# A decoder block with 32 experts on one core: how many weight tiles the experts' stage requests ahead of its products

## The chip, the cores and the metric

One core of one Trainium2 chip runs the kernel. The metric is device microseconds (us) of one execution, lower is better. The kernel before took 1326.5 us (median of 3 runs, 1325.47 to 1329.25). Five engines work side by side: TensorE (PE, matrix products), VectorE (DVE), ScalarE (ACT), GpSimd (POOL) and SyncE (SP, which here only issues transfers). Each runs its own instructions in order and waits on semaphores for the others.

## What is computed

One layer of a transformer decoder, in f32, for T = 1024 tokens of D = 1024 numbers: two kinds of attention, an output projection with a residual, and then a mixture of 32 experts. The part that matters here is the last one; cut from the reference:

```
h2 = modulate(rmsnorm(x, g_ffn), shift_ffn, scale_ffn)          # (1024, 1024)
group  = argmax(softmax(h2 @ w_group))                          # 1 of 4
top 2 of the group's 8 experts, weights p1, p2 (times the group's probability)
y[t]   = sum over the token's 2 experts e of  weight * (silu(h2[t] @ w_gate[e]) * (h2[t] @ w_up[e])) @ w_down[e]
x      = x + gate_ffn * y ;   return rmsnorm(x, g_final)
```

Each expert has three weight matrices of 1024 x 512 (gate, up) and 512 x 1024 (down), 6 MB together. Which tokens an expert gets is known only once the routing is done.

## The kernel before, in words

**The stages.** Attention takes the first 600 us or so. Then comes the out-projection with the residual and the routing (the profile shows it until about 742 us), then the experts' stage (742 to 1290 us), then the final norm. The change is in how many of the experts' weights are requested in the second of these and how many are held ahead in the third.

**The weights.** The weights of an expert are 12 tiles of 128 x 1024 numbers (512 KB): eight (`ew<e>_0` to `_7`) hold gate and up, four (`_8` to `_11`) hold down. There are 384 such tiles. The function `load_to(n)` (from L971) issues the next tiles until n of them have been requested, each with one transfer on SP's queue (L982, "ew<-we" in the profile). The tiles are requested in the order in which the products use them. For experts 4 and up the place in memory is read from a register, which SP loads first (L980).

**The slots.** Every tile is taken by `slot(name)` (L129) from one pool of `NSLOT = 49` slots of 4 KB per partition. The pool holds the weights and also the other large tiles of this stage: the gathered tokens `xe` (three, in turn), the transposed tokens `xs<e>`, the activations `sg<e>`, `act<e>`, `at<e>`, the results `ys<e>`, `yt<e>`, and the broadcast row `bc_gate2`. Slots are dealt out when the program is built, in the order in which the code asks for them. Whoever writes first into a slot waits, on the chip, until the last reader of the tile that had it before is done.

**Requests during the routing.** `end_units` lists the units of work of the out-projection stage. Between them, `spread` puts calls of `load_to`, so that after the n-th group of units `LDS[n]` tiles have been requested in all. Each of these early requests also waits for ACT's latest instruction at that place (`queue_after`, `act_now`) and for the landing of the request 14 places earlier (`PACE`).

**The experts' loop.** The token rows of the first experts are gathered by `load_x(0)`, `load_x(1)`, `load_x(2)` (GpSimd's indirect transfer, L1226). Requests made after `load_x(1)` wait for its gather. The loop then walks through a list `order` of steps: `G` e,i is the product of the i-th gate/up tile (`gate_up`, `products`), `X` e the transpose of the gathered tokens (`xpose`: PE L1259 into PSUM, then eight copies with scale and shift that ACT, L1247, and DVE, L1245, make in turn into `xs<e>`), followed by ACT's scaling of the next gathered rows (L1237), `T` e the transpose of the activations (`act_t`, PE L1310, ACT L1312), `D` e,f the product of the f-th down tile, and `Y` e the result (`finish`, DVE L1329, L1335), which GpSimd adds into memory (`add_rows`, L1342). After the last gate/up product, `gate_up` issues the activation: ACT L1295 (silu), L1282, L1300 and DVE L1296, L1283, L1301, L1302, each waiting for the one before. The list puts six of the next expert's G steps in front of X (`XA = 6`), four of them in front of T (`TA = 4`) and one between T and D (`DA = 5`). So with expert 0 the steps run: X0, G0.0 to G0.5, X1, G0.6, G0.7, G1.0 to G1.3, T0, G1.4, D0.0 to D0.3, Y0, G1.5, X2, and so on.

**The products.** An expert takes 96 rows (large) or 64 (small: 5, 7, ... 27, 30, 31). `products` multiplies the first 64 rows tile by tile (L1270). The last 32 rows of a large expert follow after every fourth tile for four tiles together (L1277), and only then are these four weight tiles given back to the pool, one after the other.

**The lead.** Before each G or D step, at position `wpos` of the 384, the loop asks for `wpos + LL` tiles, with `LL = LLX = 34` and `LT = 0`.

Of the kernel before, what the change touches and what calls it, by code (L numbers as in the profile page):

```python
# [38 lines left out]
RP, RU = 6, 0  # L39
PO = 1  # L40
PO2 = 22
LDS = [6, 6, 11, 14, 18, 22, 28, 33, 33, 34]
PACE = 14
TZ, DZ = 2, 3
W2 = [0, 0]
# [13 lines left out]
QS = "AS"  # L59
TAIL = "y s3 r0-4 o0 s4 s5 x o1 o2 s6 s7 o3 r4-9 o4 o5 o6 o7 o8"  # L60
XA, TA, DA = 6, 4, 5
LLX = 34
LT = 0
NT = 0
PLO = ()

# [29 lines left out]
def build(nc, tc, I, out, cap=CAP):  # L96
# [25 lines left out]
    def act_now():  # L122
        return next(i for i in reversed(nc.cur_bb.bb.instructions) if i.engine == mybir.EngineType.Activation)

    def queue_after(d, ins):
        tc.add_manual_dep(d.ins, ins.name, mybir.DependencyInfo(
            mybir.DependencyClass.Sync, mybir.DependencyReason.DATA), reason="order of transfers")

    def slot(name, dt=F32):  # L129
        return up.tile([128, D], dt, name=name, tag="u")  # L130

    def bank(name, shape=(128, 512)):
        return pB.tile(list(shape), F32, name=name, tag="b")
# [478 lines left out]
    def spread_row(name, col, eng):  # L612

        t = bc[name] = slot("bc_" + name)
        for h in (0, 1):
            ps = bank(f"bc_{name}{h}")
            for k in range(4 * h, 4 * h + 4):
                c = slice(k * 128, k * 128 + 128)
                if eng is A:
                    A.activation(t[:, c], ident, AF.Copy, scale=col[:, k:k + 1])  # L620
                else:
                    eng.tensor_scalar(t[:, c], ident, col[:, k:k + 1], None, op0=ALU.mult)
                PE.matmul(ps[:, c.start - h * 512:c.stop - h * 512], ones, t[:, c], start=True, stop=True)
            A.activation(t[:, h * 512:h * 512 + 512], ps, AF.Copy)
# [341 lines left out]
    wseq = [o for o in order if o[0] in "GD"]  # L966
    wpos = {o: n for n, o in enumerate(wseq)}
    loaded, after = [0], [None]

    def load_to(n):  # L970
        while loaded[0] < min(n, len(wseq)):  # L971
            kind, e, i = wseq[loaded[0]]
            c = i if kind == "G" else KT + i
            w = slot(f"ew{e}_{c}")
            cc = slice(c * 1024, (c + 1) * 1024)
            if e < NF:
                src = I["we"][e, :, cc]
            else:
                if i == 0 and kind == "G":
                    EREG[e] = nc.sync.value_load(permi[0:1, e:e + 1], min_val=0, max_val=NE - 1)  # L980
                src = I["we"][bass.ds(EREG[e], 1), :, cc].rearrange("o p c -> (o p) c")
            d = nc.sync.dma_start(w, src)  # L982
            if after[0] is None:
                queue_after(d, act_now())
                if len(fetched) >= PACE:
                    queue_after(d, fetched[-PACE])
                fetched.append(d.ins)
            else:
                queue_after(d, after[0])
                fetched.append(d.ins)  # L990
            EW[kind, e, i] = w
            loaded[0] += 1
# [53 lines left out]

    LOADS = LDS

# [176 lines left out]
    def load_x(e):  # L1225
        g = G.indirect_dma_start(out=XE[e % 3][:capof(e)], out_offset=None, in_=x1d[:],  # L1226
                                 in_offset=bass.IndirectOffsetOnAxis(ap=listof(e), axis=0),
                                 bounds_check=T - 1, oob_is_err=False)
        if e == 1:
            after[0] = g.ins  # L1230

    def scale_x(e):

        xe, c = XE[e % 3], capof(e)
        r2 = (lacc[:, 2 * NE:] if e < NF else wlP[:, NE:])[:c, e:e + 1]
        if e:
            A.activation(xe[:c], xe[:c], AF.Copy, scale=r2)  # L1237
        else:
            A.activation(xe[:c, 0:384], xe[:c, 0:384], AF.Copy, scale=r2)
            V.tensor_scalar(xe[:c, 384:1024], xe[:c, 384:1024], r2, None, op0=ALU.mult)  # L1240
# [8 lines left out]
    def xpose(e):  # L1249

        xe, c = XE[e % 3], capof(e)
        wl = lacc[:, NE:3 * NE] if e < NF else wlP
        st = ST[e] = dict(wt=wl[:c, e:e + 1],
                          x=slot(f"xs{e}")[:, :KT * c].rearrange("p (k t) -> p k t", k=KT))
        n = 512 // c // 4 * 4
        for k0 in range(0, KT, n):
            tp = bank(f"xp{e}_{k0}", (128, n, c))
            for k in range(k0, k0 + n):
                PE.transpose(tp[:, k - k0, :], xe[:c, k * 128:(k + 1) * 128], ident[:c, :c])  # L1259
            for k in range(k0, k0 + n):  # L1260
                affine(k, st["x"][:, k], tp[:, k - k0, :])
# [23 lines left out]
    def gate_up(e, k):  # L1285
        st, c = ST[e], capof(e)
        if k == 0:
            st["gu"] = wide(f"gu{e}")
        ps = st["gu"]
        products(ps, st["x"], e, "G", k, KT)  # L1290
        if k == KT - 1:
            act = st["act"] = slot(f"act{e}")[:, 0:512]
            tmp = slot(f"sg{e}")
            s = tmp[64:128, 0:512]
            A.activation(s, ps[0:64, 0:512], AF.Silu)  # L1295
            V.tensor_mul(act[0:64], s, ps[64:128, 0:512])  # L1296
            if c > 64:
                t, s = tmp[0:64, 0:512], tmp[32:64, 512:1024]
                others(t, ps)
                A.activation(s, t[0:32], AF.Silu)  # L1300
                V.tensor_mul(act[64:96], s, t[32:64])  # L1301
            V.tensor_scalar(act[:c], act[:c], st["wt"], None, op0=ALU.mult)  # L1302
            del st["gu"]

    def act_t(e):
        st, c = ST[e], capof(e)
        act = st.pop("act")
        tp = bank(f"ap{e}", (128, 4, c))
        for f in range(4):
            PE.transpose(tp[:, f, :], act[:c, f * 128:(f + 1) * 128], ident[:c, :c])  # L1310
        st["a"] = slot(f"at{e}")[:, 0:4 * c].rearrange("p (k t) -> p k t", k=4)
        A.activation(st["a"], tp, AF.Copy)  # L1312

    def down(e, f):
        st = ST[e]
        if f == 0:
            st["y"] = wide(f"y{e}")
        products(st["y"], st["a"], e, "D", f, 4)

    def finish(e):  # L1320
        st, c = ST.pop(e), capof(e)
        ps = st["y"]
        p0 = 64 if e == NE - 1 else 0
        ys = YL if e >= NE - 2 else slot(f"ys{e}")
        g = bc["gate2"]
        halves = [(slice(h * 512, h * 512 + 512), h) for h in (0, 1)]
        for n, h in halves:
            r = slice(h * 64, h * 64 + 64)
            V.tensor_mul(ys[p0:p0 + 64, n], ps[r, 0:512], g[r, n])  # L1329
        if c > 64:  # L1330
            t = slot(f"yt{e}")[0:64, 0:512]
            others(t, ps)
            for n, h in halves:
                r = slice(h * 32, h * 32 + 32)
                V.tensor_mul(ys[64:96, n], t[r], g[r, n])  # L1335
        if e < NE - 2:
            add_rows(e, ys)
        if e == NE - 3:
            f_load()
# [22 lines left out]
    def f_square(tt, x):  # L1362
        FY[tt] = slot(f"fy{tt}")
        A.activation(FY[tt], x, AF.Square, accum_out=ssf[:, tt:tt + 1])
# [8 lines left out]
            G.indirect_dma_start(out=out[:], out_offset=rows_l, in_=y, in_offset=None,  # L1373
                                 bounds_check=T - 1, oob_is_err=False)

    LL = LLX
    load_x(0)
    load_x(1)
    load_x(2)
# [6 lines left out]
    for o in order:  # L1386
        kind, e, i = o
        if kind in "GD":
            load_to(max(loaded[0], wpos[o] + LL - wpos[o] * LT // len(wseq)))
        if kind == "G":  # L1390
            gate_up(e, i)
        elif kind == "X":
            xpose(e)
            if e + 1 < NE:
                scale_x(e + 1)
            if e + 2 < NE:
                load_x(e + 2)
        elif kind == "T":
            act_t(e)
        elif kind == "D":  # L1400
            down(e, i)
        elif kind == "Y" and e < NE - 1:
            finish(e)
        if o == ("G", NE - 3, 4):

            spread_row("final", cols[:, 72:80], G)
            XL, YL = slot("xlast"), slot("ylast")
            ML = slot("same")[:, 0:128]
            G.memset(XL, 0.0)
            A.activation(ML, ident, AF.Copy, scale=lsLf)  # L1410
            mp = bank("same", (128, 128))
            PE.matmul(mp, ones, ML, start=True, stop=True)
            V.tensor_scalar(ML, mp, lsLf, None, op0=ALU.is_equal)
        if e == NE - 1 and kind == "D" and i:
            f_square(i - 1, FX[i - 1])
# [37 lines left out]
    with tc.If(rv > 0):  # L1453
# [5 lines left out]
        for tt in range(KT):  # L1459
            for c in (0, 1):  # L1460
                o, j, ov = wk[:, 0:32], wk[:, 32:64], wk[:, 64:65]
# [135 lines left out]
```

## Time and profile before

| | |
|---|---|
| Runs | 1325.47, 1326.5, 1329.25 us; median 1326.5 |
| Profiled execution, its own time | 1328.25 us |
| Its span in the trace | 1326.5 us |
| Granted PE clock, mean | 0.960 |
| PE busy | 1168.2 us, 88% of the span |
| DVE, ACT, POOL busy | 738.0, 530.5, 227.1 us |
| Transfers | 304.8 MB, mean 230 GB/s over the span |
| Experts' weights | 384 transfers of 512 KB, median 10.8 us to landing |

"Span" is the time between the first and the last instruction in the trace; the execution's own time is 1.75 us longer. In the chain that ended last, PE has 43% and DMA 23% of the span. A row "A <- B: x, n, y" of the waits says that A stood idle for x us in n waits, y the longest, each ended by B. In the timeline a row gives start, duration, engine, line, operation, out<-in, count, and in brackets the engine's idle time before it and what ended it. In the windows' rows, PEclk is the clock granted to PE as a share of full speed, and "DMA share" the mean busy share of the core's 16 DMA engines.

### The profile page before, as it was taken

The page shows a single profiled execution, that of the slowest core. Times are in us where ns is not written, and L with a number is a line of the kernel's source. Part 1 is how long each engine was busy: PE and PEld are TensorE (multiplying, and loading weights), DVE is VectorE, ACT ScalarE, POOL GpSimd, SP SyncE. Part 2 cuts the span into 40 slices and gives each one's busy share as a digit, 9 for nine tenths or more (in the row PEclk, how much of TensorE's full clock was granted, in tenths as well). Part 3 has the DMA queues.
Part 4 walks back from the last instruction along what each step waited for, and adds up shares of the span by engine and source line. Part 5 has one row for each costly group of instructions (what it writes and reads, how often), then busy time and mean ns, then how long its engine had stood idle before and what let it go on. Part 6 is the DMA issues. An engine that isn't in the chain of part 4 may idle for free.

```text
span 1326.5 us, 19360 instructions
## 1 busy us (share of the span) xinstructions
PE 1168.2 (88%) x6810; PEld 686.3 (52%) x6810; DVE 738.0 (56%) x1433; ACT 530.5 (40%) x1080; POOL 227.1 (17%) x275
## 2 busy tenths in 40 slices
PE   4699989999999999699887999899999998888872
PEld 3497778778866887487666422223233322222220
DVE  6958773865497848968866243333333333323225
ACT  5346553666555445434634432232222222222312
POOL 3600010110100002222323111111111111111200
PEclk9799999999999999899999899999999999999986
DMA  9423442431001010356767899999999999999984
GB/s 350 169 69 97 153 159 90 149 60 69 24 25 48 17 64 1 126 208 225 250 219 273 303 318 367 339 387 373 370 375 375 370 371 369 368 386 379 387 332 175
DMA packets 89432, 304.80 MB, mean 230 GB/s; under 512 B 12402, under 2 KB 14834, under 8 KB 89330
## 3 DMA queue, kind: packets, MB, share of 16 engines
q1 hardware_dynamic: 81778, 282.00, 57.7%
q0 software_dynamic: 6400, 17.31, 5.3%
q10 hardware_dynamic: 1152, 4.19, 0.8%
q8 instruction: 56, 0.92, 0.3%
q14 instruction: 46, 0.38, 0.1%
HBM read 278.56 MB, written 29.63 MB: 232 GB/s over the span
## 4 chain that ended last, share of the span: by engine, by line
PE 43%; DMA 23%; DVE 22%; ACT 7%; issue 4%; POOL 1%; SPq 0%; POOLq 0%; DVEq 0%; ACTq 0%
DMA ew<-we 21%; PE gu L1270 5%; PE y L1270 4%; PE o L572 4%; DVE K L531 3%; DVE wada L209 2%; PE tp L548 2%; PE op L665 2%; PE op L667 2%; PE op L666 2%; DMA wada<-w_adaT 2%; PE y L1277 2%; DVE P L513 2%; PE pv L459 2%; PE pv L460 2%
## 5 line engine op out<-in xcount | busy, mean ns | idle before, releaser
L1270 PE MATMUL gu<-ew,xs 128*64 128x512 f32 x1024 | 251.6, 610 | 13.3 <-DMA ew<-we 9.8
L1329 DVE TENSOR_TENSOR ys<-y,bc_gate 64x512 f32<-64x512 f32 x60 | 41.3, 688 | 208.5 <-PE y L1277 120.8
L1270 PEld LDWEIGHTS gu<-ew,xs 128*64 128x64 f32 x1024 | 62.8, 136 | 147.3 <-issue 68.6
L1270 PE MATMUL y<-ew,at 128*64 128x512 f32 x512 | 124.5, 618 | 11.2 <-DMA ew<-we 10.0
L1247 ACT ACTIVATE xs<-xp,modc,affn 128x96 f32<-128x96 f32 (+1 forms) x128 | 51.6, 418 | 148.8 <-PE xp L1259 76.4
L548 PE MATMUL tp<-ident,P 128*128 128x128 f32 x576 | 89.0, 280 | 19.4 <-DVE P L532 9.6
L1342 POOL DMA_INDIRECT acc<-ys,lsP x26 | 37.2, 1433 | 369.4 <-DVE ys L1335 255.4
L531 DVE TENSOR_TENSOR_SCAN K<-K 128x1024 f32<-128x1024 f32 (+7 forms) x64 | 92.8, 1451 | 5.9 <-ACT K L519 5.7
L515 ACT ACTIVATE P<-P,st 128x1024 f32<-128x1024 f32 (+7 forms) x64 | 49.8, 778 | 90.2 <-DVE st L513 45.7
L548 PEld LDWEIGHTS tp<-ident,P 128*128 128x128 f32 x576 | 65.8, 141 | 38.1 <-issue 9.7
L1270 PEld LDWEIGHTS y<-ew,at 128*64 128x64 f32 x512 | 36.3, 142 | 95.1 <-issue 48.0
L572 PE MATMUL o<-PT,v 128*64 128x256 f32 (+1 forms) x640 | 75.1, 375 | 9.4 <-DVE PT L553 5.7
L1245 DVE TENSOR_SCALAR xs<-xp,affn,modc 128x96 f32<-128x96 f32 (+1 forms) x128 | 45.4, 362 | 59.0 <-ACT xs L1247 58.4
L519 ACT ACTIVATE K<-S 128x1024 f32<-128x1024 f32 (+7 forms) x64 | 41.8, 653 | 73.4 <-PE S L502 34.4
L1277 PE MATMUL gu<-ew,xs 128*32 128x512 f32 x576 | 70.9, 611 | 0.0
L209 DVE CUSTOM_DVE_ANT_0 wada<-wada,sc 128x1024 f32<-128x1024 f32 x48 | 64.4, 1353 | 9.6 <-DMA wada<-w_adaT 9.5
L513 DVE CUSTOM_DVE_ANT_0 P<-S,B 128x1024 f32<-128x1024 f32 (+7 forms) x64 | 48.2, 755 | 35.9 <-PE S L500 31.4
L1282 ACT ACTIVATE yt<-y 64x512 f32<-64x512 f32 x18 | 10.7, 593 | 143.1 <-PE xp L1259 111.9
L572 PEld LDWEIGHTS o<-PT,v 128*64 128x64 f32 x640 | 45.6, 141 | 39.5 <-DVE PT L553 8.2
L551 ACT ACTIVATE PT<-tp 128x512 f32<-128x512 f32 (+3 forms) x120 | 56.1, 495 | 14.8 <-PE tp L548 14.0
L532 DVE TENSOR_TENSOR P<-P,K 128x1023 f32<-128x1023 f32 (+7 forms) x64 | 51.5, 805 | 5.7 <-ACT P L520 0.8
L553 DVE COPY PT<-tp 128x512 f32<-128x512 f32 (+3 forms) x72 | 37.3, 536 | 17.8 <-PE tp L548 17.4
(641 smaller groups left out, 2507.3 us busy)
## 6 DMA issues: line engine op xcount, KB each, us to landing
ew<-we SPq DMA_DIRECT2D x384, 512.0 KB, 10.8
wada<-w_adaT SPq DMA_DIRECT2D x48, 512.0 KB, 5.7
wqk<-wqk SPq DMA_DIRECT2D x16, 512.0 KB, 3.9
xT<-xT SPq DMA_DIRECT2D x16, 256.0 KB, 5.3
wv<-wv SPq DMA_DIRECT2D x8, 512.0 KB, 7.6
B<-bias SPq DMA_DIRECT2D x8, 512.0 KB, 5.4
wo<-w_out SPq DMA_DIRECT2D x8, 512.0 KB, 5.0
x<-x SPq DMA_DIRECT2D x8, 512.0 KB, 4.2
```

Source lines behind the costliest of these rows:

```text
L209: V.tensor_tensor_reduce(w, w, sc, op0=ALU.mult, op1=ALU.add, scale=1.0, scalar=0.0, accum_out=modc[:, v * 8 + k:v * 8 + k + 1])
L513: V.tensor_tensor_reduce(e, s, Bt[p, hd][:, :L], op0=ALU.add, op1=ALU.min, scale=-0.125, scalar=BIG, accum_out=st[:, 0:1])
L515: A.activation(e, e, AF.Exp, bias=st[:, 0:1], scale=-1.0, accum_out=st[:, 2:3])
L531: V.tensor_tensor_scan(k[:, :L], k[:, :L], k[:, :L], 1.0, op0=ALU.mult, op1=ALU.bypass)
L532: V.tensor_mul(b[:, 1:L], b[:, 1:L], k[:, 0:L - 1])
L548: PE.transpose(tp[:, jl - 4 * x, :], e[:, (jl - qo) * 128:(jl - qo) * 128 + 128], ident)
L551: A.activation(dst, tp[:, j0 - 4 * x:j1 - 4 * x, :], AF.Copy)
L572: PE.matmul(ps[hd * 64:hd * 64 + 64, 0:w], VV[p][:, j, hd * 64:hd * 64 + 64], pt[hd][jl // 4][:, jl % 4, 0:w], start=(n == 0), stop=(n == ...
L1245: V.tensor_scalar(dst, src, affn[:, k:k + 1], modc[:, 24 + k:25 + k], op0=ALU.mult, op1=ALU.add)
L1247: A.activation(dst, src, AF.Identity, scale=affn[:, k:k + 1], bias=modc[:, 24 + k:25 + k])
L1270: PE.matmul(ps[h * 64:h * 64 + 64, 0:512], a[:, i, 0:64], w[:, h * 512:h * 512 + 512], start=(i == 0), stop=(i == n - 1))
L1277: PE.matmul(ps[r:r + 32, 512:1024], a[:, j, 64:96], w[:, h * 512:h * 512 + 512], start=(j < 2), stop=(j >= n - 2))
```

## The change

Two tables change. In `LDS` more tiles are requested by each group of units of the routing stage, 43 instead of 34 in all. In the experts' loop the lead at position p is max(43 - p // 7, 34): 43 at the first step, one less at every seventh, 34 from p = 63 on. The line `LL = LLX` goes, so that the lines below stand one or two higher (L1247 is L1246, L982 is L981).

```diff
-LDS = [6, 6, 11, 14, 18, 22, 28, 33, 33, 34]
+LDS = [12, 12, 15, 18, 22, 25, 31, 39, 42, 43]
...
-LLX = 34
-LT = 0
+LLX, LLD = (43, 34), 7
...
-    LL = LLX
...
-            load_to(max(loaded[0], wpos[o] + LL - wpos[o] * LT // len(wseq)))
+            load_to(max(loaded[0], wpos[o] + max(LLX[0] - wpos[o] // LLD, LLX[1])))
```

The instructions of PE, ACT, DVE and POOL and their order are the same in both programs. What differs is SP's order, the slots, and with them the waits.

SP's queue, in the first units of the out-projection stage, before. (L117 loads a part of the residual stream, `x1_<t>`; L942 stores one, `x1d<-x1_<t>`; the names' last numbers count the tiles in the order in which the program asks for them; in brackets, the engines and queues that the instruction waits for.)

```order
L117 DMA x1_7_5527<-acc_305 128x1024 [waits DMAHW4_49,DMAHW1_49]
L982 DMA ew0_0_5608<-we 128x1024 [waits DMAHW6_49,DMAHW2_49,Activation_49]
L982 DMA ew0_1_5610<-we 128x1024
L982 DMA ew0_2_5612<-we 128x1024 [waits PE_49]
L942 DMA x1d_310<-x1_6_5525 128x1024 [waits DMAHW5_49,DMAHW0_49,DVE_49]
L982 DMA ew0_3_5634<-we 128x1024 [waits DMAHW7_49,DMAHW6_49,PE_49]
L982 DMA ew0_4_5636<-we 128x1024 [waits PE_49]
L982 DMA ew0_5_5638<-we 128x1024 [waits DMAHW1_49,PE_49]
L117 DMA x1_4_5654<-acc_305 128x1024 [waits DMAHW2_49]
L942 DMA x1d_310<-x1_7_5527 128x1024 [waits DMAHW4_49,DVE_49]
L117 DMA x1_5_5840<-acc_305 128x1024 [waits DMAHW5_49,DVE_49,Activation_49]
```

The same place now:

```order
L116 DMA x1_7_5527<-acc_305 128x1024 [waits DMAHW4_49,DMAHW1_49]
L981 DMA ew0_0_5608<-we 128x1024 [waits DMAHW6_49,DMAHW2_49,Activation_49]
L981 DMA ew0_1_5610<-we 128x1024
L981 DMA ew0_2_5612<-we 128x1024 [waits PE_49]
L981 DMA ew0_3_5614<-we 128x1024 [waits DMAHW5_49,PE_49]
L981 DMA ew0_4_5616<-we 128x1024 [waits PE_49]
L981 DMA ew0_5_5618<-we 128x1024 [waits DMAHW7_49,PE_49]
L941 DMA x1d_310<-x1_6_5525 128x1024 [waits DMAHW1_49,DMAHW0_49,DVE_49]
L981 DMA ew0_6_5640<-we 128x1024 [waits DMAHW2_49,DMAHW0_49,PE_49]
L981 DMA ew0_7_5642<-we 128x1024 [waits DMAHW3_49,PE_49]
L981 DMA ew1_0_5644<-we 128x1024 [waits DMAHW4_49]
L981 DMA ew1_1_5646<-we 128x1024 [waits DMAHW5_49,PE_49]
```

Twelve tiles instead of six now stand ahead of the load of `x1_4` (it follows two rows after the last one shown). Further down, from `ew3_5` (the 42nd tile) on, SP's queue has the same transfers in the same order in both programs.

ACT at the start of the experts' stage, before: X0's copies into `xs0`, the scaling of expert 1's gathered rows, X1's copies into `xs1`, the scaling of expert 2's.

```order
L1247 ACTIVATE xs0_7007<-xp0_0_7008,modc_93,affn_95 128x96 [waits PE_49]
L1247 ACTIVATE xs0_7007<-xp0_0_7008,modc_93,affn_95 128x96 [waits DVE_49]
L1247 ACTIVATE xs0_7007<-xp0_4_7017,modc_93,affn_95 128x96 [waits PE_49]
L1247 ACTIVATE xs0_7007<-xp0_4_7017,modc_93,affn_95 128x96 [waits DVE_49]
L1237 ACTIVATE xe1_6762<-xe1_6762,lacc_320 96x1024 [waits DMASW1_49]
L1247 ACTIVATE xs1_7058<-xp1_0_7059,modc_93,affn_95 128x96 [waits DMAHW6_49,DMAHW5_49,PE_49]
L1247 ACTIVATE xs1_7058<-xp1_0_7059,modc_93,affn_95 128x96 [waits DVE_49]
L1247 ACTIVATE xs1_7058<-xp1_4_7068,modc_93,affn_95 128x96 [waits PE_49]
L1247 ACTIVATE xs1_7058<-xp1_4_7068,modc_93,affn_95 128x96 [waits DVE_49]
L1237 ACTIVATE xe2_6764<-xe2_6764,lacc_320 96x1024 [waits DMASW2_49]
```

And now:

```order
L1246 ACTIVATE xs0_7025<-xp0_0_7026,modc_93,affn_95 128x96 [waits PE_49]
L1246 ACTIVATE xs0_7025<-xp0_0_7026,modc_93,affn_95 128x96 [waits DVE_49]
L1246 ACTIVATE xs0_7025<-xp0_4_7035,modc_93,affn_95 128x96 [waits PE_49]
L1246 ACTIVATE xs0_7025<-xp0_4_7035,modc_93,affn_95 128x96 [waits DVE_49]
L1236 ACTIVATE xe1_6774<-xe1_6774,lacc_320 96x1024 [waits DMASW1_49]
L1246 ACTIVATE xs1_7085<-xp1_0_7086,modc_93,affn_95 128x96 [waits PE_49]
L1246 ACTIVATE xs1_7085<-xp1_0_7086,modc_93,affn_95 128x96 [waits DVE_49]
L1246 ACTIVATE xs1_7085<-xp1_4_7095,modc_93,affn_95 128x96
L1246 ACTIVATE xs1_7085<-xp1_4_7095,modc_93,affn_95 128x96 [waits DVE_49]
L1236 ACTIVATE xe2_6776<-xe2_6776,lacc_320 96x1024 [waits DMASW2_49]
```

The instructions are the same. The first copy into `xs1` waited for two hardware DMA queues and for PE, now for PE alone; the third one, which reads the second half of the transposes, waited for PE and now waits for nothing. A semaphore that an engine has already seen at a later count is not waited for again.

SP's queue at the same point of the program, now. (Before, `xs1_7058` is asked for between `ew2_9_7054` and `ew2_10_7081`, the 39th and 40th tile.)

```order
L979 TENSOR_LOAD permi_315 [waits DVE_49]
L979 ISA x2
L981 ISA
L981 DMA ew4_0_7052<-we 128x1024 [waits DMAHW4_49,PE_49]
L981 ISA
L981 DMA ew4_1_7065<-we 128x1024 [waits DMAHW5_49,PE_49]
L981 ISA
L981 DMA ew4_2_7077<-we 128x1024 [waits DMAHW6_49,PE_49]
L981 ISA
L981 DMA ew4_3_7081<-we 128x1024 [waits DMAHW7_49,PE_49]
L981 ISA
L981 DMA ew4_4_7108<-we 128x1024 [waits DMAHW0_49,PE_49]
```

By the names' numbers `xs1_7085` is now asked for between `ew4_3_7081` and `ew4_4_7108`, the 48th and 49th tile.

## Rows read from the trace of the kernel before

**Rows 1.** The page: busy time, share of the span and instructions of each engine.

```profile
PE 1168.2 (88%) x6810; PEld 686.3 (52%) x6810; DVE 738.0 (56%) x1433; ACT 530.5 (40%) x1080; POOL 227.1 (17%) x275
```

**Rows 2.** The chain that ended last, in order of time, its longest pieces in the experts' stage: start us, us, what.

```profile
742.53 3.65 PE gu L1270 x16
...
932.20 3.43 PE y L1270 x16
946.88 16.05 DMA ew<-we
...
1235.29 7.88 DMA ew<-we
1243.70 3.58 PE y L1270 x16
```

**Rows 3.** Busy time of each engine in stretches of the experts' stage: us, busy (x instructions) of PE, PEld, DVE, ACT and POOL, PEclk, DMA share, GB/s.

```profile
742.00:780.00 38.00, 36.78 (x225) 11.30 (x224) 12.85 (x25) 14.43 (x25) 3.47 (x3) 1.00 0.93 320
...
820.00:860.00 40.00, 36.38 (x206) 11.44 (x204) 14.74 (x26) 9.88 (x19) 4.81 (x4) 0.96 0.98 352
...
1100.00:1150.00 50.00, 41.75 (x222) 11.35 (x220) 14.03 (x28) 12.35 (x23) 7.25 (x6) 1.00 1.02 363
```

**Rows 4.** Waits of SP's queue from 742 to 800 us, and then from 866 to 1245 us.

```profile
SPq L982 <- PE gu L1277: 20.0, 6, 6.1
...
SPq L982 <- DMA acc<-ys,ls: 7.6, 2, 4.4
...
SPq L982 <- DMA ew<-we: 228.3, 240, 3.2
```

**Rows 5.** Waits of PE from 742 to 860 us, and then from 946 to 1245 us.

```profile
PE ap L1310 <- DVE act L1302: 6.4, 4, 3.4
...
PE y L1270 <- DMA ew<-we: 10.0, 13, 1.8
PE gu L1270 <- DMA ew<-we: 9.8, 11, 2.4
```

**Rows 6.** Transfers issued from 742 to 866 us, and then from 866 to 1245 us: count, size, median us from issue to landing.

```profile
ew<-we SPq DMA_DIRECT2D x79, 512.0 KB, 7.7
...
ew<-we SPq DMA_DIRECT2D x245, 512.0 KB, 12.4
```

**Rows 7.** SP's requests in order of time: the first four after 742 us, and the next one.

```profile
747.21 2.74 SPq L982 DMA_DIRECT2D ew<-we  x4
...
753.64 0.34 SPq L982 DMA_DIRECT2D ew<-we  x1
```

**Rows 8.** PE in order of time around X1 and T0.

```profile
749.84 0.88 PE L1259 MATMUL xp<-ident,xe 96*128 96x96 f32 x8
...
752.52 1.92 PE L1277 MATMUL gu<-ew,xs 128*32 128x512 f32 x16
...
759.89 0.55 PE L1310 MATMUL ap<-ident,act 96*128 96x96 f32 x4
```

**Rows 9.** ACT and DVE in order of time from X1's first copy to expert 0's activation.

```profile
750.43 0.43 ACT L1247 ACTIVATE xs<-xp,modc,affn 128x96 f32<-128x96 f32 x1 [4.83 <-PE xp L1259]
...
752.84 1.14 ACT L1237 ACTIVATE xe<-xe,lacc 96x1024 f32<-96x1024 f32 x1
753.99 1.28 ACT L1295 ACT_TABLE_LOAD   x1
755.28 0.59 ACT L1295 ACTIVATE sg<-gu 64x512 f32<-64x512 f32 x1
...
759.35 0.48 DVE L1302 TENSOR_SCALAR act<-act,lacc 96x512 f32<-96x512 f32 x1
```

**Rows 10.** PE, ACT and DVE in order of time around X2 and T1.

```profile
770.35 1.92 PE L1277 MATMUL gu<-ew,xs 128*32 128x512 f32 x16
...
778.73 0.55 PE L1310 MATMUL ap<-ident,act 96*128 96x96 f32 x4 [1.02 <-DVE act L1302]
...
771.44 0.75 ACT L1247 ACTIVATE xs<-xp,modc,affn 128x96 f32<-128x96 f32 x2 [2.12 <-DVE xs L1245]
...
771.03 0.38 DVE L1245 TENSOR_SCALAR xs<-xp,affn,modc 128x96 f32<-128x96 f32 x1
```

**Rows 11.** PE in order of time: T3 with the down products after it, and then T4 with its own.

```profile
816.40 0.55 PE L1310 MATMUL ap<-ident,act 96*128 96x96 f32 x4 [1.01 <-DVE act L1302]
...
823.18 1.08 PE L1270 MATMUL gu<-ew,xs 128*64 128x512 f32 x4
...
835.61 0.66 PE L1310 MATMUL ap<-ident,act 96*128 96x96 f32 x4 [3.41 <-DVE act L1302]
844.03 1.08 PE L1270 MATMUL gu<-ew,xs 128*64 128x512 f32 x4
```

**Rows 12.** The stretch after that wait, in the columns of rows 3.

```profile
835.90:839.30 3.40, 3.40 (x12) 1.09 (x11) 0.00 (x0) 0.49 (x1) 0.00 (x0) 0.50 1.00 377
```

**Rows 13.** The first gather's landing as DVE sees it, ACT's first use of it, and the first gathers' median us to landing among the transfers from 725 to 745 us, then from 866 to 1245 us.

```profile
735.46 0.55 DVE L1240 TENSOR_SCALAR xe<-xe,lacc 96x640 f32<-96x640 f32 x1 [0.52 <-DMA xe<-x1d,ls]
...
739.88 0.60 ACT L1239 ACTIVATE xe<-xe,lacc 96x384 f32<-96x384 f32 x1
...
xe<-x1d,ls POOLq DMA_INDIRECT x4, 4.9
...
xe<-x1d,lsP POOLq DMA_INDIRECT x22, 8.2
```

## The prediction

> **What bounds the kernel now.** I read the page first, then the chain that ended last in order of time, then the experts' stage in stretches, then the waits of SP and PE by stage. PE is the busiest engine over the whole span [rows 1], but the reader should look at the stage that the change touches, and at what ends last there. The chain goes along PE's products from 742.53 to 946 us, then along the landing of weights until 1245, then along PE again [rows 2]. So the experts' stage has two regimes.
>
> In the early one PE is nearly always busy, 36.78 of 38 us [rows 3]. It does not wait for weights at all: its waits from 742 to 860 us are for DVE's activation in front of the transposes T, 6.4 us in four waits [rows 5]. SP is the one that is held up: it waits for PE to give tiles back, 20.0 us in six waits for one line alone [rows 4]. The pool is full, and every request follows PE's pace.
>
> In the later regime it is the other way round. SP waits for earlier transfers to land, 228.3 us of 379 [rows 4], and PE waits 19.8 us for weights in 24 waits [rows 5]. A tile takes 379 us / 245 = 1.55 us [rows 6]. In the early regime 79 tiles went in 124 us, 1.57 us each [rows 6]: slightly slower, because of the slots.
>
> A time in the early regime therefore counts fully. What PE loses there, the requests lose with it, and the later regime starts that much later.
>
> **What the change adds.** Nine more tiles are to be held when the products begin. But there are 49 slots. Before, at the step X1 (in front of it, position 5 asks for 5 + 34) 39 tiles had been asked for; now 5 + 43 = 48. Four have been given back by then (`ew0_0` to `ew0_3`), three slots hold gathered rows, one the broadcast row and one `xs0`. Before, that made 39 - 4 + 5 = 40 of 49, so nine were free; now it makes 48 - 4 + 5 = 49, none.
>
> *The tiles.* With 49 slots, the first request that has to wait for PE's giving back was the 42nd (four requests at 747.21 to 749.95, then the next at 753.64 [rows 7]); now it is the 45th, since only three slots had been left over. So three of the nine tiles really come earlier. From position 63 on the lead is 34 in both, and the requests wait for the same steps of PE. PE does not wait for weights before 860 us [rows 5], so three tiles that land earlier there shorten nothing: worth 0 us in my sum. The transfers in the later regime would profit only if the three tiles' worth of transfers stayed ahead, 3 x 1.55 = 4.6 us; as the lead is given back by position 63, I take 0 and keep 4.6 as the other end.
> The Trainium skill ("DMA: Bandwidth & Descriptors", Rules for kernel authors) advises to issue a transfer early and to wait for it late; by that rule alone the nine tiles would be worth up to 9 x 1.55 = 14 us. No row of the early regime shows a wait of PE that an earlier landing would end [rows 5], so the sum goes without it.
>
> *The slot of xs1.* This is the cost. With no free slot at X1, `xs1` must take the next slot to be given back, and that is `ew0_4`'s. Before, it had one left from the routing stage (its first copy waited for two DMA queues beside PE); now it waits for a PE instruction that lies behind both halves of X1's transposes, as the third copy no longer waits at all. PE finishes the transposes at 750.72, and ACT's first copy started at 750.43 [rows 8, 9]. `ew0_4` is read last by the second group of products L1277, which starts at 752.52 [rows 8]; the request at 753.64, which waits for the same tile, shows when it is given back [rows 7]. The first copy is late by 753.64 - 750.43 = 3.2 us. Behind it everything is in series: the eight copies that ACT and DVE make in turn, ACT's scaling at 752.84, the table load, the silu at 755.28, and the rest up to DVE's last step, 759.35 + 0.48 = 759.83 [rows 9]. PE starts T0 at 759.89 with no idle time before it [rows 8], so nothing is in hand: **+3.2 us** of waiting on PE. Queued behind the waiting copy on ACT and DVE are only these same steps; POOL's next gather waits for X1's chain as well, but its rows are needed an expert later.
>
> *The slot of xs2.* At X2 (position 17) 17 + 43 - 2 = 58 tiles have been asked for, 16 given back, and the pool is full again; `xs2` gets `ew1_4`'s slot. The group L1277 that reads it last starts at 770.35 [rows 10]; with the same 1.12 us as above it is given back at 771.47. ACT's first copy then starts at 771.47, and DVE's first behind its 0.43 us [rows 9], at 771.90. Before, that copy ran at 771.03, held by DVE's own work [rows 10]. That is **+0.9 us** on T1, where PE already waited 1.02 us [rows 10]. From X3 on the slots that `xs` takes are given back earlier than the copies need them; 0 us.
>
> *The clock.* The wait of 3.41 us at T4 was followed by a stretch at a granted clock of 0.50, the 1.2 GHz level [rows 11, 12]. From T to the end of the down products took 844.03 - 835.61 = 8.42 us there, and 823.18 - 816.40 = 6.78 at T3, after a wait of 1.01 us and at full clock [rows 11]. The new wait of 3.2 us is nearest to T4's, so I add the difference, **+1.6 us**. T1's wait would be 1.9 us, between the two; I take nothing for it, and 1.6 us as the other end.
>
> *The routing stage.* More tiles are in flight while the first rows are gathered. The gather of expert 0 landed at 735.46 and ACT needed it at 739.88, 4.4 us later [rows 13]. A gather took 4.9 us there and takes 8.2 us in the full regime [rows 13]: 3.3 us more, hidden under the 4.4. If that cover were gone, each further microsecond would count fully. SP's loads and stores of the residual stream are moved behind three to six more requests; SP's requests are spread over the stage, and I take 0.
>
> **Sum.** 3.2 + 0.9 + 1.6 = +5.7 us. The profiled execution took 1328.25 us, 1.75 above its median; I carry the difference over: 1326.5 + 5.7 = **1332.2 us** (the profiled execution would become 1333.9, its span 1332.2). Without the clock's term it is 1330.6, with it at T1 as well 1333.8. Could transfers catch up? By their pace, at most 79 x (1.57 - 1.55) = 1.6 us; I take 0, since their requests wait for the same late steps. With both savings the low end of this case is 1329.0.
>
> **Rivals.**
> - *Nothing to see.* `xs1` waits for a tile that is given back in time, such as `ew0_0` to `ew0_3` (747.21 to 749.95, before 750.43 [rows 7, 9]), and then the change only does a third of what it says. T0 stays, T1 loses at most 0.9: 1326.5 to 1327.4 us. For it speaks that the new order of waits doesn't name the tile; against it, that the wait covers both halves of the transposes, which end after 749.95. It decides at 750.43.
> - *Faster: the early tiles carry through.* If the transfers' head start of three tiles is still there when the transfers become the bound, everything from 946 us on comes 4.6 us earlier, 1321.9 us; this needs `xs1`'s wait to be hidden as well, or the two nearly cancel (1327.6). For it: the later regime is bound by landings, for 300 us [rows 2]. Against it: the lead of the two programs is the same from position 63 on, and DMA share was 0.93 and 0.98 in the early regime already [rows 3]. It decides whether SP's requests near 866 us come before or after their old times.
> - *Slower still: the gathers.* Eight tiles more in front of a gather would delay it by 8 x 1.55 = 12.4 us; less the 4.4 in hand, 8.0 us, and 1340.2 us in all. Against it: rows that share the engines with weights took 8.2 us in the median, not 17 [rows 13]. The Trainium skill ("DMA: Bandwidth & Descriptors", Issuing engines are not separate DMA queues) says that transfers of different engines run on the same 16 DMA engines and interleave. By that the gathers would be slowed but not queued behind all the tiles, and the +3.3 us above are the likelier size.
>
> **How the numbers follow.** The forecast's own mechanism has 0.55, nothing to see 0.26, faster 0.12, gathers 0.07. A measurement of this kernel can tell about 0.3% from no change, 4.0 us, so slower begins at 1330.5. Of the forecast's 0.55 I put 0.07 under that bound (a clock that stays up, transfers that catch up): slower 0.48 + 0.07 = 0.55, same 0.26 + 0.07 = 0.33, faster 0.12. The range leaves out the faster and the gathers' case and reaches from the lowest run of the no-change case, 1325.4, to 1333.8 plus the 1.0 by which runs lie apart, 1334.8. The likeliest case alone has 1329.0 to 1334.8.
>
> **What would show it.** Right: ACT's first copy into `xs1` starts about 3.2 us after the transposes instead of beside them, with PE's L1277 as what it waited for; PE idles some 3.2 us in front of T0 and 1.9 in front of T1; a stretch at clock 0.50 follows T0; SP's requests from about 860 us on come 5 to 6 us later; PE's waits for weights in the later regime stay near 20 us. Wrong: no idle time before T0, or a first product of the experts later than 742.5, or requests near 866 us that come earlier than before.

## The result, and the profile after

The changed kernel takes 1333.85 us (median of 20 runs, 1328.03 to 1338.59), the kernel before 1325.74 us in 20 runs of the same comparison (1320.42 to 1329.25). The ratio is 1.0068, 95% interval [1.0052, 1.0084]: slower by 6.9 to 11.1 us. The profiled execution's span is 1335.0 us against 1326.5. (In the run e11 below one execution took 4891 us, far from all others; it is left out of that run's ratio.)

The place where it happens is the one that the prediction named. ACT and DVE in order of time around X1 and T0 in the changed kernel, to be held against [rows 9]:

```profile
753.99 0.43 ACT L1246 ACTIVATE xs<-xp,modc,affn 128x96 f32<-128x96 f32 x1 [8.03 <-PE gu L1276]
...
756.40 1.14 ACT L1236 ACTIVATE xe<-xe,lacc 96x1024 f32<-96x1024 f32 x1
757.55 1.28 ACT L1294 ACT_TABLE_LOAD   x1
758.85 0.59 ACT L1294 ACTIVATE sg<-gu 64x512 f32<-64x512 f32 x1
...
762.91 0.48 DVE L1301 TENSOR_SCALAR act<-act,lacc 96x512 f32<-96x512 f32 x1
```

The reader is to see the bracket of the first row. Before, the first copy into `xs1` was released by the transposes (PE xp). Now it has waited 8.03 us instead of 4.83, and what released it is PE's second pass over the weights, L1276. SP's next request goes out at the same moment, since it waited for the same group of products (SP's queue in the same kernel; compare the request at 753.64 in [rows 7]):

```profile
754.04 1.17 SPq L981 DMA_DIRECT2D ew<-we  x2
```

Everything behind it on ACT and DVE is later by the same amount, and PE waits. PE in order of time: the first product, X1 to the products behind T0, T1, expert 2's down products, and T4 (for [rows 8, 10, 11]):

```profile
742.90 3.65 PE L1269 MATMUL gu<-ew,xs 128*64 128x512 f32 x16
...
750.21 0.88 PE L1258 MATMUL xp<-ident,xe 96*128 96x96 f32 x8
...
752.89 1.92 PE L1276 MATMUL gu<-ew,xs 128*32 128x512 f32 x16
...
763.45 0.90 PE L1309 MATMUL ap<-ident,act 96*128 96x96 f32 x4 [3.20 <-DVE act L1301]
764.28 1.98 PE L1269 MATMUL gu<-ew,xs 128*64 128x512 f32 x4
766.04 5.42 PE L1269 MATMUL y<-ew,at 128*64 128x512 f32 x16
771.39 1.92 PE L1276 MATMUL y<-ew,at 128*32 128x512 f32 x16
773.24 1.08 PE L1269 MATMUL gu<-ew,xs 128*64 128x512 f32 x4
...
786.20 0.55 PE L1309 MATMUL ap<-ident,act 96*128 96x96 f32 x4 [1.91 <-DVE act L1301]
...
808.91 3.65 PE L1269 MATMUL y<-ew,at 128*64 128x512 f32 x16 [0.59 <-ACT at L1311]
...
845.70 0.90 PE L1309 MATMUL ap<-ident,act 96*128 96x96 f32 x4 [3.48 <-DVE act L1301]
```

T0 waits 3.20 us and T1 1.91 us. The products behind T0 ran at half the clock for longer than those behind T4 did before: 763.45 to 773.24 is 9.79 us, against 6.78 at full clock and 8.42 behind T4 [rows 11]. The windows (us, busy of PE, PEld, DVE, ACT, POOL, PEclk, DMA share, GB/s) behind T0 and behind T1 show the granted clock:

```profile
764.00:769.90 5.90, 5.90 (x17) 1.77 (x17) 0.00 (x0) 0.49 (x1) 0.00 (x0) 0.52 0.61 242
769.90:773.00 3.10, 3.10 (x24) 0.70 (x20) 0.00 (x0) 0.00 (x0) 0.00 (x0) 1.00 0.00 0
786.70:791.30 4.60, 4.60 (x15) 1.44 (x16) 0.00 (x0) 0.49 (x1) 0.00 (x0) 0.63 0.47 151
```

Almost 6 us at 0.52, close to the 1.2 GHz level, and behind it the transfers stand still (0 GB/s): SP's next request waits 7.6 us, until 772.48, for the pass L1276 behind the down products, which gives tiles back. The early regime (the first two rows; compare [rows 3]) has lost DMA share as well as PE time, the later one (the third row) has not:

```profile
742.00:780.00 38.00, 34.68 (x193) 10.94 (x193) 9.86 (x20) 10.67 (x19) 2.77 (x3) 0.91 0.68 231
...
820.00:860.00 40.00, 35.45 (x188) 10.80 (x188) 14.23 (x25) 10.35 (x18) 3.83 (x5) 0.91 0.95 326
...
1100.00:1150.00 50.00, 44.97 (x240) 12.57 (x239) 15.82 (x29) 11.90 (x24) 6.34 (x6) 1.00 1.02 388
```

The waits of PE from 742 to 860 us, then from 946 to 1245 us ([rows 5]). In the later stretch PE waits 13.7 us for weights, where it was 19.8:

```profile
PE ap L1309 <- DVE act L1301: 10.7, 5, 3.5
PE y L1269 <- ACT at L1311: 0.6, 1, 0.6
...
PE y L1269 <- DMA ew<-we: 8.6, 9, 2.5
...
PE gu L1269 <- DMA ew<-we: 5.1, 4, 1.6
```

The sum of the offsets can be read from the starts of the transposes T. Since the first product falls at slightly different times in every execution, each is taken from the first product (742.53 before, 742.90 after):

| Start, us after the first product | T0 | T1 | T2 | T3 | T4 | T5 |
|---|---|---|---|---|---|---|
| before | 17.4 | 36.2 | 55.0 | 73.9 | 93.1 | 110.9 |
| changed | 20.6 | 43.3 | 63.9 | 83.5 | 102.8 | 121.8 |
| later by | 3.2 | 7.1 | 8.8 | 9.7 | 9.7 | 10.9 |

Step by step: 3.2 us of waiting at T0; 3.9 by T1 (0.9 of waiting and 3.0 of clock); 1.7 by T2 (clock behind T1); 0.8 by T3; 1.2 by T5 (a longer stretch of half clock behind T4's wait; the wait itself was there before). From T5 to T15 nothing is added: 277.5 against 266.5 us, 11.0. The last of the 384 requests goes out 538.9 us after the first product instead of 528.9 (at 1281.8 and 1271.4 us), 10.0 later.

### The profile page after: what moved, and what is told of

It is laid out like the page before. It is cut to its first block, busy times and chain, and to the rows that moved or that the text cites. A ratio compares the mean times of both kernels' runs of the same rounds, so it can differ in the third digit from the quotient of the medians.

```text
span 1335.0 us, 19366 instructions
## 1 busy us (share of the span) xinstructions
PE 1178.8 (88%) x6810; PEld 691.9 (52%) x6810; DVE 737.5 (55%) x1433; ACT 531.1 (40%) x1080; POOL 226.3 (17%) x275
## 4 chain that ended last, share of the span: by engine, by line
PE 35%; DMA 32%; DVE 18%; issue 6%; ACT 5%; POOL 1%; SPq 0%; POOLq 0%; ACTq 0%; DVEq 0%
DMA ew<-we 29%; PE o L571 4%; DVE K L530 3%; PE tp L547 2%; PE y L1269 2%; DVE wada L208 2%; PE op L664 2%; PE op L666 2%; PE op L665 2%; PE pj L415 2%; PE pj L416 2%; PE pj L417 2%; PE pv L458 2%; PE pv L460 2%; PE pv L459 2%
## 5 line engine op out<-in xcount | busy, mean ns | idle before, releaser
L1269 PE MATMUL y<-ew,at 128*64 128x512 f32 x512 | 131.4, 646 | 11.0 <-DMA ew<-we 8.6
L1246 ACT ACTIVATE xs<-xp,modc,affn 128x96 f32<-128x96 f32 (+1 forms) x128 | 51.8, 419 | 156.8 <-PE xp L1258 83.9
L518 ACT ACTIVATE K<-S 128x1024 f32<-128x1024 f32 (+7 forms) x64 | 41.8, 653 | 73.9 <-PE S L501 35.7
L1276 PE MATMUL gu<-ew,xs 128*32 128x512 f32 x576 | 69.3, 598 | 0.0
L1281 ACT ACTIVATE yt<-y 64x512 f32<-64x512 f32 x18 | 10.7, 594 | 147.0 <-PE xp L1258 104.9
## 6 DMA issues: line engine op xcount, KB each, us to landing
ew<-we SPq DMA_DIRECT2D x384, 512.0 KB, 11.1
```

Source lines behind the costliest of these rows:

```text
L1246: A.activation(dst, src, AF.Identity, scale=affn[:, k:k + 1], bias=modc[:, 24 + k:25 + k])
L1269: PE.matmul(ps[h * 64:h * 64 + 64, 0:512], a[:, i, 0:64], w[:, h * 512:h * 512 + 512], start=(i == 0), stop=(i == n - 1))
L1276: PE.matmul(ps[r:r + 32, 512:1024], a[:, j, 64:96], w[:, h * 512:h * 512 + 512], start=(j < 2), stop=(j >= n - 2))
```

## The experiments

Two theories. **Slots**: the requests fill the pool, so `xs1` and `xs2` wait for a weight tile that PE is still using; that wait and the half clock behind it are the loss. **Crowding**: the requests themselves cost, by delaying gathers, the first product or later transfers.

**One tile less.**

```diff
-LLX, LLD = (43, 34), 7
+LLX, LLD = (42, 34), 7
```

> The lead starts at 42 instead of 43, one tile less at X1; xs1 then takes the slot of ew0_3, which is given back about 750.0, and xs2 that of ew0_11. Theory slots (xs1 and xs2 wait for a tile of the current group): no wait in front of T0, 1.0 us in front of T1, no stretch at half clock behind them, time as before, ratio to before 0.998 to 1.003 (about 1326). Theory crowding (the nine more requests themselves cost: they delay the gathers, the first product or the transfers): nearly all of it stays, ratio 1.005 to 1.007 (about 1333).

Measured: 1323.25 us against 1324.1 before, ratio 0.9994 [0.9979, 1.0008]. The whole loss is gone with one tile of nine. ACT at X1, and PE at T0 and T1:

```profile
750.30 0.43 ACT L1246 ACTIVATE xs<-xp,modc,affn 128x96 f32<-128x96 f32 x1 [4.84 <-PE xp L1258]
...
759.76 0.55 PE L1309 MATMUL ap<-ident,act 96*128 96x96 f32 x4
...
778.61 0.55 PE L1309 MATMUL ap<-ident,act 96*128 96x96 f32 x4 [1.03 <-DVE act L1301]
```

The copy is released by the transposes again, as in [rows 9], and T0 has no wait. Crowding would have kept eight ninths of the loss. It also says what the tiles held ahead are worth by themselves: eight more requests, at most 0.2% either way.

**Only the early requests, only the loop.** The changed kernel with one of the two tables set back. In e2 it is the loop's lead (the first edit), in e3 the early requests (the second):

```diff
-LLX, LLD = (43, 34), 7
+LLX, LLD = (34, 34), 7
...
-LDS = [12, 12, 15, 18, 22, 25, 31, 39, 42, 43]
+LDS = [6, 6, 11, 14, 18, 22, 28, 33, 33, 34]
```

> Only the routing stage requests more (43), the lead in the loop is 34 as before. Theory slots: 43 requested at X1, five slots free, no wait at T0; the time of before, ratio 0.998 to 1.003; the first product some 0.4 us later as after the change. Theory crowding: 43 tiles are in flight or landed when the first gathers run, so the loss is here: ratio 1.005 to 1.007.

> Only the lead in the loop is changed (43 falling to 34), the routing stage requests 34 as before. Theory slots: 48 requested at X1 as after the change, xs1 takes the slot of ew0_4, T0 waits 3.2 us, T1 1.9 us, with half clock behind them: ratio 1.005 to 1.008 (1333 to 1336). Theory crowding of the routing stage: as before, 0.998 to 1.003.

Measured: 1.0011 [0.9993, 1.0028] for the early requests, 1.0086 [1.0059, 1.0113] for the loop's lead. The 43 early requests cost nothing that can be measured; the number asked for at X1 (5 + 43 in both the loop's version and the change) costs all of it. The first product of e2 came at 740.42 us, not 0.4 us later than before as expected. In e3, PE at T0 and T1:

```profile
762.60 0.55 PE L1309 MATMUL ap<-ident,act 96*128 96x96 f32 x4 [3.20 <-DVE act L1301]
784.03 0.59 PE L1309 MATMUL ap<-ident,act 96*128 96x96 f32 x4 [1.91 <-DVE act L1301]
```

**xs1's slot alone.** All requests stay as changed; `xs1` is given its slot before the loop (`XS` is a dictionary, empty at first).

```diff
+    XS[1] = slot("xs1")
+    G.memset(XS[1][:, 0:1], 0.0)
     xpose(0)
...
-                          x=slot(f"xs{e}")[:, :KT * c]...
+                          x=(XS.pop(e) if e in XS else slot(f"xs{e}"))[:, :KT * c]...
```

> The changed kernel, but xs1 gets a slot before the loop starts (GpSimd writes one column of it), so that a weight tile waits for ew0_4 instead of xs1; all other slots of the first experts are as after the change. Theory slots: T0's wait of 3.2 us and the half clock behind it (3.0 us) are gone, T1's 1.9 us and the clock behind it stay: ratio to before 1.001 to 1.004 (1327 to 1331), some 5 us under the changed kernel. Theory crowding: no gain, 1.005 to 1.008.

Measured: 1.0043 [1.0025, 1.006], 1328.41 us. T0's wait is gone (0.07 us) and T1's stays at 1.98 us; by T5 the profile is 1.9 us behind before's (112.8 against 110.9 us from the first product), of which 1.0 is T1's wait and 0.8 the step at T3. So the slot of `xs1` is worth a third of the loss in the time if it is held against the changed kernel's 1.0068, half if against e3's 1.0086 from the same chip, and more than that in the profile. The ratio lies above what the profile shows, by some 4 us. The profiled execution, 1326.51 us, is the shortest of the seven (up to 1332.9); see also e11 below.

**A larger dose.**

```diff
-LLX, LLD = (43, 34), 7
+LLX, LLD = (45, 34), 7
```

> The changed kernel with a lead that starts at 45: xs1 takes the slot of ew0_6, xs2 that of ew1_6. In the group of products that gives four tiles back one after the other, these are two tiles later, 2 x 0.48 = 1.0 us each. Theory slots: T0 waits 4.2 us, T1 2.9 us; 1.9 us more than the changed kernel, ratio to before 1.007 to 1.010. Rival (the wait is hidden behind the weights, and the loss comes from elsewhere): as the changed kernel, 1.006 to 1.007.

Measured: 1.0158 [1.0134, 1.0181], 1340.42 us: worse by more than either theory said. T0 came 4.0 us later than before from the first product, near the 4.2 expected, but T1 waited 6.57 us. The chain of expert 1 on ACT and DVE shows a new place; then PE at T1:

```profile
780.75 0.59 ACT L1294 ACTIVATE sg<-gu 64x512 f32<-64x512 f32 x1
785.32 0.69 DVE L1295 TENSOR_TENSOR act<-sg,gu 64x512 f32<-64x512 f32 x1 [5.22 <-DMA acc<-ys,ls]
786.04 0.59 ACT L1281 ACTIVATE sg<-gu 64x512 f32<-64x512 f32 x1 [4.70 <-DVE act L1295]
...
789.30 0.90 PE L1309 MATMUL ap<-ident,act 96*128 96x96 f32 x4 [6.57 <-DVE act L1301]
```

DVE's first write into `act1` waited for GpSimd's addition of expert 0's result to land: in this program `act1` has the slot that `ys0` had. The sign and the growth with the dose fit the slots; the size was taken from two waits only, where a third came up.

**Slots without requests.** The kernel before, with nine slots taken by nothing from X0 to X2.

```diff
+    HOLD = [slot(f"hold{i}") for i in range(9)]
+    for h in HOLD:
+        G.memset(h[:, 0:1], 0.0)
...
             xpose(e)
+            if e == 2:
+                for h in HOLD:
+                    G.memset(h[:, 0:1], 0.0)
```

> The kernel before (34 tiles requested early, lead 34) with nine slots of the pool held by nothing until X2 (GpSimd writes one column of each before X0 and after X2). No further tile is requested, but xs1 takes the slot of ew0_4 and xs2 that of ew1_6. Theory slots: T0 waits 3.2 us, T1 some 2.9 us, half clock behind them: ratio to before 1.006 to 1.011, as much as the change or more. Rival (the requests cost, not the slots): as before, 0.998 to 1.003.

Measured: 1.0106 [1.0084, 1.0128], 1335.63 us, with not one request more than before:

```profile
753.28 0.43 ACT L1247 ACTIVATE xs<-xp,modc,affn 128x96 f32<-128x96 f32 x1 [8.02 <-PE gu L1277]
...
762.74 0.90 PE L1310 MATMUL ap<-ident,act 96*128 96x96 f32 x4 [3.20 <-DVE act L1302]
787.78 0.55 PE L1310 MATMUL ap<-ident,act 96*128 96x96 f32 x4 [2.68 <-DVE act L1302]
```

The same 3.20 us at T0, and 2.68 at T1 (some 2.9 expected). With e1, e3 and e7 the cause of the sign is settled: it is the full pool.

**The half clock.** Idle products in front of T0 and T1, where PE waits anyway (`warm(n)` issues 4n products of 128x128).

```diff
+FILL = {0: 10, 1: 5}
...
+            warm(FILL.get(e, 0))
             act_t(e)
```

> The changed kernel with idle products in front of T0 (40 of 128x128, some 3.0 us) and T1 (20, some 1.5 us), in place of PE's waiting. T0 and T1 start when they did. Theory: of the loss at T0 and T1, 3.0 and 1.7 us are the half clock behind the waits and go away; 4.7 us less than the changed kernel, ratio to before 1.002 to 1.005. Rival (the half clock is a consequence and costs nothing at the end, since the weights decide it): as the changed kernel, 1.006 to 1.008.

> The changed kernel once more, on one chip with the two below, so that their ratios share the runs of the kernel before: 1.006 to 1.009; by the first product, T5 starts some 11 us later than before, as in its first profile.

> The changed kernel with the idle products of the run e6_fill, beside the changed kernel itself. Theory (the half clock behind T0 and T1 costs what it holds PE up): T5 some 6 us earlier than in the changed kernel by the first product, and 3 to 6 us in the time, a ratio 0.002 to 0.0045 under the changed kernel's. Rival (the half clock costs nothing at the end): the ratio of the changed kernel within 0.001.

Measured: e6 1.0055 [1.0041, 1.007]; then on one chip the changed kernel again (e9), 1.0064 [1.0033, 1.0095] with T5 at 121.6 us from the first product, and the idle products (e10), 1.0049 [1.0029, 1.007] with T5 at 114.5. In e6's profile T0 stands where it stood (20.6 us), PE's wait is filled and the clock stays up (the down products take 3.60 us, not 5.42):

```profile
761.50 2.41 PE L262 MATMUL scr<-onesb 128*128 128x128 bf16 x40
764.77 0.55 PE L1310 MATMUL ap<-ident,act 96*128 96x96 f32 x4 [0.86 <-DVE act L1302]
...
766.15 3.60 PE L1270 MATMUL y<-ew,at 128*64 128x512 f32 x16
...
782.52 1.29 PE L262 MATMUL scr<-onesb 128*128 128x128 bf16 x20
784.51 0.55 PE L1310 MATMUL ap<-ident,act 96*128 96x96 f32 x4 [0.69 <-DVE act L1302]
```

T1 comes 40.3 us after the first product instead of 43.3, T2 59.2 instead of 63.9: the 3.0 and the 1.7 us are there, and are the clock's. But in the time the idle products save 0.0013 and 0.0015, about 2 us, in both comparisons; the intervals overlap each time. By the medians of e9 and e10, 1333.9 and 1329.88, it is 4.0 us. So neither the expected 3 to 6 us nor the rival's zero is shown. Every execution has its mean granted clock on record. In e10 it is 0.960 on average, as in the kernel before (0.960), in e9 0.956. Of the 20 executions of the changed kernel, the four shortest (1328.0 to 1328.7 us) have 0.960 to 0.963, and the five with 0.954 or less took 1336.2 to 1337.9 us. The time goes with the clock, then, but these means do not say which stretch was slow. What the half clock behind T0 and T1 costs in the time stays open between 0 and some 4 us.

**T1 filled, with xs1's slot ahead.** e4 with `FILL = {1: 5}`.

> The run e4_xs_first (xs1 has its slot ahead) with 20 idle products in front of T1, where PE waited 1.98 us. If that run's 1.0043 is more than its profile shows (1.8 us by T5) because the clock falls behind T1 in other executions, this one is lower: 1.000 to 1.003. If it comes from elsewhere, 1.003 to 1.006.

Measured: 1.0015 [0.9995, 1.0035], where e4 had 1.0043 [1.0025, 1.006]. In e4's profile the clock stayed at 1.00 behind T1's wait of 1.98 us, in the changed kernel's it fell to 0.63 behind 1.91 us. The lower ratio fits a clock that falls there in some executions. But the two come from different comparisons, their intervals overlap, and in e4 the longest execution (1332.9 us) has a higher mean clock than the shortest, 0.959 against 0.957; it is not shown.

**The other direction.** The kernel before, with X two steps earlier, so that PE's waits of [rows 5] in front of T1 to T4 go away.

```diff
-XA, TA, DA = 6, 4, 5
+XA, TA, DA = 4, 4, 5
```

> The kernel before with X of the expert after the next put between T and D (XA = 4 instead of 6), so that its copies run on ACT and DVE while PE makes the down products, and DVE's work on the result no longer stands in front of them. Theory (time of PE in the early regime counts fully): the waits of 1.0 us at T1 to T3 and of 3.4 us at T4 with the half clock behind it go, up to 8 us by T5; ratio to before 0.994 to 0.998. Rival (the later regime is bound by the transfers and takes the gain back): 0.998 to 1.002.

Measured: 1.0005 [0.9989, 1.0021]. The waits did go (PE's from 742 to 860 us, then its waits for weights from 946 to 1250 us):

```profile
PE ap L1310 <- DVE act L1302: 1.1, 1, 1.1
...
PE gu L1270 <- DMA ew<-we: 17.8, 22, 2.0
PE y L1270 <- DMA ew<-we: 8.3, 8, 1.9
```

From the first product, T5 comes at 101.7 us instead of 110.9 and T15 at 252.0 instead of 266.5, but T20 at 344.6 against 343.7: PE runs ahead until it meets the landing weights, and waits 26.1 us for them instead of 19.8. The time is the rival's. The profile agrees only in part: the last request goes out 524.9 us after the first product, 4.0 earlier than before, and the end comes after 575.5 us, where it took 584.0 before and 581.5 and 581.0 in e1 and e2. The first product of this execution was late, at 746.98 us, and 3.2 us of that are there already when the first gather goes out (733.99 instead of 730.83 us). So most of the gain is lost by T20, some of it is there at the end of this one profile, and none could be measured in the time.

## Why the prediction was right, point by point

- **What bounds.** Right for a loss: by T5 the changed kernel is 10.9 us late from the first product, and its last request is 10.0 us late. From the first product to the end its two profiles took 592.1 and 591.9 us, e1 and e2, whose early regime is before's, 581.5 and 581.0: 10.7 us. Before's own profile took 584.0, so against it the end is late by 8.1 us, which is also the difference of the medians. So between nothing and 2.8 us was made up; the 1.6 us allowed for catching up can be neither confirmed nor ruled out. "A time in the early regime counts fully" was too wide, though: in e8 PE was 9.2 us earlier by T5, and the time did not change. In the early regime the transfers ran at a share of 0.93 and 0.98 already [rows 3]. PE's delay takes requests from them; that PE's lead gives them little to be faster with is the likely reason for e8, and e8's profile shows it in part.
- **The tiles: 0 us.** Right. e1 and e2 hold eight and nine more tiles at the start and gain nothing. The advice of the Trainium skill ("DMA: Bandwidth & Descriptors", Rules for kernel authors) to issue early, by which alone it would have been up to 14 us, does not bear on a stage where no product waits for a landing.
- **The slot of xs1: +3.2.** Right, to the hundredth: 3.20 us.
- **The slot of xs2: +0.9.** Right: T1's wait is 1.91 instead of 1.02. The Trainium skill ("Perfetto Trace Analysis", Optimization Strategy) says that a gap that keeps coming can mean that there is no room in SBUF for the next tile. The trace agrees only in part: the short-lived `xs` is left without room, but its gaps are two, of 3.20 and 1.91 us. The gap that does keep coming, 1.0 us at T1 to T3, was there before, with nine slots free at X1, and went away in e8 with the order of the steps.
- **The clock: +1.6.** The mechanism was right and the size off. It was taken from one stretch behind one wait. In the profile it came to 3.0 behind T0, 1.7 behind T1 (for which I took nothing) and 1.2 more behind T4. This term, with `at2` below, makes the difference between the sum's 5.7 and the profile's 10.9. In the time, e6 and e10 put its part behind T0 and T1 at about 2 us, and leave it open.
- **Missed: at2.** The step at T3, +0.8 us, is a third tile without room. Its row in the changed kernel (in e1, as before, what it waited for was PE's transposes):

```profile
808.37 0.49 ACT L1311 ACTIVATE at<-ap 128x384 f32<-128x384 f32 x1 [2.89 <-DMA acc<-ys,ls]
```

  `at2` now has the slot of `ys1` and waits for the addition of expert 1's result to land. The prediction looked at `xs` alone.
- **The gathers: 0.** Nearly right. They took 9.5 us in the median instead of 4.9 [rows 13], and the 4.4 us in hand were used up:

```profile
739.26 0.55 DVE L1239 TENSOR_SCALAR xe<-xe,lacc 96x640 f32<-96x640 f32 x1 [5.36 <-DMA xe<-x1d,ls]
...
739.60 0.61 ACT L1238 ACTIVATE xe<-xe,lacc 96x384 f32<-96x384 f32 x1 [0.64 <-DMA xe<-x1d,ls]
```

  ACT waited 0.64 us, not 8. The gathers were 4.6 us longer, near the 3.3 that were taken and far from the rival's 12.4 for a gather queued behind the tiles.
- **The signs.** ACT's first copy, the idle times at T0 and T1 and the half clock behind T0 came as stated. Two signs did not. The requests were to come 5 to 6 us later from about 860 us on, and the 109th came 11.1 us later (126.3 instead of 115.2 us after the first product), since the early loss is about twice the sum. PE's waits for weights were to stay near 20 us and fell to 13.7. And the first product came at 742.90 us, later than the 742.5 named as a sign of being wrong; as it falls anywhere from 740.2 to 747.0 us in these profiles, that sign decides nothing.
- **The time.** 1332.2 was forecast and 1333.85 measured, inside 1329.0 to 1334.8. That it lies inside is luck in part. With the 10.9 us of the profile at T5 in place of 5.7 the sum would have been 1337.4; the measured loss was 8.1 us, on a kernel before that took 1325.74 this time instead of 1326.5.

## What to carry to other kernels

A prefetch depth that uses up the last slot of a shared pool moves the wait from the transfer queue, where it cost nothing here, to whichever small tile asks next; count what else the pool must hold at each step, and stop one tile short (42 cost nothing, 43 cost 0.7%, 45 cost 1.6%). Before deepening a prefetch, look whether any consumer waits for a landing in that stage at all. And where a stage bound by PE feeds one bound by transfers, do not count a gain in the first like a loss in it: here 10.9 us lost by T5 were 8.1 us in the time, and 9.2 us gained by T5 were nothing that could be measured.

## What the runs showed of the hardware that was not expected

- The same wait of PE does not always have the same price. T4's wait was 3.41 to 3.48 us in all of these profiles but e8's, and from T4 to T5 it took 16.2 us in e10, 17.8 before and in e6, and 19.0 in the changed kernel. In e10 the clock never fell behind that wait:

```profile
840.00:846.00 6.00, 5.29 (x28) 1.86 (x32) 0.62 (x2) 0.49 (x1) 0.00 (x0) 1.00 1.03 384
```

  Before, it was 0.50 in the stretch behind the wait [rows 12]. So 0, 1.6 or 2.9 us follow the same wait, and one profiled stretch is a poor price for it.
- The first product falls between 740.2 and 747.0 us after the start in these profiles; the changed kernel alone has 742.90 and 745.46 in its two. A few microseconds of a single profile's span come from before the stage that is compared; starts are better taken from a common event.
